# Moving all adaLN modulations to VectorE and regrouping attention into items of two score tiles

## The chip, the cores and the metric

The kernel runs on one core of one Trainium2 chip. The metric is the device time in microseconds (us) of one execution. TensorE (PE, with its weight loads as PEld), VectorE (DVE), ScalarE (ACT) and GpSimd (POOL) compute; SyncE (SP) issues the transfers from HBM.

## What is computed

One residual block on 256 tokens of width 1024 (a mixture of HGRN2, mLSTM and Mamba-2 branches, then a gated feed-forward with a depthwise convolution), a final norm, and then two layers of a second block on a latent stream of 256 tokens and a context stream of 256 tokens. All is float32. What matters here is the second block's modulation and its attention:

```python
def modulation(cond, w_ada, b_ada):
    m = jax.nn.silu(cond) @ w_ada + b_ada
    return [t[..., None, :] for t in jnp.split(m, 6, axis=-1)]

s_win = jnp.einsum('bnqhgd,bnkhd->bnhgqk', qb, kb).astype(jnp.float32) * scale
s_win = jnp.where(valid[None, :, None, None], s_win, -jnp.inf)
p = jax.nn.softmax(jnp.concatenate([s_win, s_ctx, s_sink], axis=-1), axis=-1)

p = jax.nn.softmax(s, axis=-1)
pd = p[:, :, 0] - lam * p[:, :, 1]
return jnp.einsum('bhqk,bkhd->bqhd', pd.astype(v.dtype), v)
```

The modulation of a layer is a product of two condition rows (one for the latent stream, one for the context) with a 1024 x 6144 matrix. The first softmax is that of 8 window heads of width 64 with 2 key heads, with a learned sink in the denominator; the last three lines are the 4 differential heads, each with two score maps of width 32 and values of width 64.

## The kernel before, in words

**Products.** Every weight tile (128 partitions x 1024 float32, 512 KB) is loaded by a transfer on SP's queue into the pool `wraw` of 4 buffers (`weight_raw`, L376), rounded on ScalarE to a high part `wh` (L383) and subtracted on VectorE to a low part `wl` (L385); both parts have 3 buffers. TensorE then makes the product in three passes (high x high L404, low activations L406, low weights L407; L429 to L431 for the projections that put tokens on partitions): 24 matmuls of 256 columns per weight in most stages. The scheduler orders each engine's instructions ahead of time, by the place in the program and with gaps filled by later work that is ready; buffers of a pool are handed out in program order, and a weight's load waits on SP's queue until the buffer that it takes is free. So the loads of the shared pool stand in the order of the program.

**Modulations.** A generator makes them in steps, and `ada_tick`, called after each weight (L417, L433, L634), runs one step each `pace` ticks. For layer 0 they are made on TensorE (`ada_pe`, L541 and L542): 12 blocks of 512 columns by 4 weights, each weight an ordinary `weight` (load, cast, subtract) and four matmuls of 512 columns with the condition rows as the stationary operand, then copies and small transposes (L528). They run from the mLSTM and SSD stage (`pace1` 2, set at L1190) through the first block's feed-forward (`pace3` 5, L1312), and what is left is run by `ada_rest()` behind that feed-forward (L1335). For layer 1, 40 blocks of 128 columns are made on VectorE (`ada_dve`, L571 to L582) during layer 0's feed-forward at `pace2` 1: a load into a pool of its own (`araw`, 3 buffers), and per condition one multiply-and-sum over 1024 elements (L580). Two blocks of 512 columns are left for TensorE, as filler in layer 1's attention (`afill`, L1677). `ada_rest()` stands behind layer 0's feed-forward too (L1728).

**Attention.** For each tile of 128 queries there are 12 items: 8 window heads, then 4 differential heads. `scores` runs two items ahead, `transposed` one ahead, and `values` last. A window head's scores are three matmuls over 64 array rows (L1517 to L1519) into a PSUM bank, with a mask matmul of 256 columns for latent tiles (L1521); then a maximum (L1523), a scaled maximum (L1525 or L1527), an exponential with sum (L1529), four transposes (L1562), a copy (L1564) and four products with the transposed probabilities as the stationary operand and 128 value columns of both key heads, of which 64 are used (L1574). A float32 matmul shows as two instructions in the trace. A differential head has two maps of 32 array rows, whose probabilities are combined (L1556). Latent tiles see 512 keys, context tiles 256. `OB` gathers the results with tokens on partitions; `finished` transposes six blocks of it and splits them into `XH` and `XL`. In layer 0 the context tiles run beside projections and the latent tiles beside the context's output products (`fill` says behind which items); in layer 1 only latent tiles remain.

Of the kernel before, what the change touches and what calls it, by code (L numbers as in the profile page):

```python
# [28 lines left out]
# columns of the modulations done on the tensor engine, 512 at a time, and on the vector engine, 128  # L29
ADA = ((range(0, 6144, 512), range(0)), (range(5120, 6144, 512), range(0, 5120, 128)))  # L30
# [3 lines left out]
# column offsets of the first block's w_in  # L34
# [4 lines left out]
# rows of the small projections: i gates, f gates, dt  # L39
# [3 lines left out]
def _ws(name, layer, c0, nk=8, r0=0):  # L43
    """[nk*128, 128] block of a weight, rows on partitions, 128 columns."""
    def cut(w):
        return w[name][layer][r0:r0 + nk * 128, c0:c0 + 128].reshape(nk, 128, 128).transpose(1, 0, 2)
    return nk * 128, cut


def _xs(name, layer, c0, half, cols=None):  # L50
    """[512, 256] block: rows on partitions, 256 columns that stream."""
    def cut(w):
        a = w[name][layer][half * 512:(half + 1) * 512]
        a = a[:, c0:c0 + 256] if cols is None else a[:, cols]
        return a.reshape(4, 128, 256).transpose(1, 0, 2)
    return 1024, cut


def _ada(layer, c0, q):
    """[256, 512] block: rows on partitions, 512 columns."""  # L60
    def cut(w):
        a = w["w_ada_2"][layer][q * 256:(q + 1) * 256, c0:c0 + 512]
        return a.reshape(2, 128, 512).transpose(1, 0, 2)
# [24 lines left out]
def _qcols(c):  # L88
    """256 columns of the window attention's queries, heads j and j + 4 side by side."""
    return np.concatenate([np.arange(512 + 64 * h, 576 + 64 * h) for h in HEADORDER[4 * c:4 * c + 4]])  # L90

# [33 lines left out]
def plan2(layer):  # L125
    p = [(("ada", c0, q), _ada(layer, c0, q)) for c0 in ADA[layer][0] for q in range(4)]
    p += [(("adat", c0), _adat(layer, c0)) for c0 in ADA[layer][1]]
# [8 lines left out]
    p += [(("out", j), _ws("w_out_2", layer, 128 * j)) for j in range(8)]  # L136
# [140 lines left out]
class Knobs:  # L277
    raw = 4
    wh = 3
    wl = 3  # L280
    big = 9
    araw = 3
# [17 lines left out]
def tile_two_blocks(ctx: ExitStack, tc: tile.TileContext, xT, ctxT, cst1, cst, cstw, pb1, pl0, pl1, pf0, pf1, pc, pcb, wb, w0, w1, out,  # L300
# [16 lines left out]
    class PS:  # L317
        """PSUM pools of the phase at hand"""

    def psum(**bufs):  # L320
        """Shares out the eight banks: name=number."""
# [3 lines left out]
        for nm in "asgcpo":  # L325
            if nm not in bufs:
                setattr(PS, nm, None)

    psum(g=3, s=4, a=1)
# [30 lines left out]
    ones = const.tile([128, 128], F32, name="ones")  # L360
    V.memset(ones, 1.0)
    onesn = const.tile([128, 128], F32, name="onesn")
# [30 lines left out]
    def gained(dst_h, dst_l, x, g):  # L393
        """x g, split: what the first products after a norm take; 1 / rms is applied to their results"""
# [4 lines left out]
    def mm3(o, w, rhs, nk, late=False, first=True, last=True):  # L399
        """o = W^T x in three passes; late: the low part of x comes last."""  # L400
# [11 lines left out]
    def gemm_ws(ph, key, rhs, n, nk=8, late=False, w=None):  # L412
        """out[128 features, n tokens] = W^T x; rhs(k) gives (high, low)."""
        w = w or weight(ph, key, 128)
        ps = PS.g.tile([128, 512], F32, tag="g", name="psg")
# [4 lines left out]
    def gemm_xs(ph, keys, lhs, toks, evac):  # L420
        """out[128 tokens, 256 features]; lhs(k, t) gives (high, low) of a token tile."""
        w = [weight(ph, k, 256) for k in keys]
        for t in toks:
            ps = PS.g.tile([128, 512], F32, tag="g", name="psx")
# [11 lines left out]
    def rsqrt_raw(pool, a, n, tag, bufs, rows=128):  # L436
        """RS * result = 1 / sqrt(a)"""
# [3 lines left out]
        # in two halves, so that neither waits for the step before  # L441
# [13 lines left out]
    def mean_sq(x, scale=None, eps=EPS):  # L455
        """mean of squares + eps, [128 tokens, 2 blocks of them], in PSUM"""
# [20 lines left out]
    def rms_all(a):  # L477
        """[128, 256] on every partition: 1 / (RS sqrt(a)) for tokens on partitions"""
# [19 lines left out]
    # =====================================================================  # L498
    # modulation: silu(c) w + b for both conditions, features on partitions
    # =====================================================================  # L500
    mods = [res.tile([128, 48, 2], F32, name="mod%d" % i) for i in range(2)]

    class Ada:
        pool = rows = None
# [5 lines left out]
    def ada_prep():  # L510
        zp = ctx.enter_context(tc.tile_pool(name="zp", bufs=1))
        Ada.cs = zp.tile([128, 8, 2], F32, name="ccs")
        Ada.cr = zp.tile([128, 8, 4], F32R, name="ccr")
        ct2 = zp.tile([128, 8, 2], F32, name="ct2")
        nc.sync.dma_start(out=ct2.rearrange("p k c -> p (k c)"), in_=pc)
        Ada.pf = [load_params(zp, _pf(i), (pf0, pf1)[i], "pf%d" % i) for i in range(2)]
        th = zp.tile([128, 8, 2], F32, name="cth")
        S.activation(out=th, in_=ct2, func=AF.Tanh, scale=0.5)
        V.scalar_tensor_tensor(th, th, 1.0, ct2, ALU.add, ALU.mult)
        V.tensor_scalar(Ada.cs, th, 0.5, None, ALU.mult)  # L520
        split(Ada.cr[:, :, 0:2], Ada.cr[:, :, 2:4], Ada.cs)

    def ada_pe(li):
        """512 columns at a time on the tensor engine; both parts of the conditions share a pass."""
        def finish(c0, rows):
            pt = PS.s.tile([128, 4, 4], F32, tag="s", name="psat")
            for q in range(4):
                T.transpose(pt[:, q], rows[q // 2][0:4, q % 2 * 128:q % 2 * 128 + 128], ident[0:4, 0:4])  # L528
            o = slice(c0 // 128, c0 // 128 + 4)
            V.tensor_tensor(mods[li][:, o], pt[:, :, 0:2],  # L530
                            Ada.pf[li]("bada")[:, o].unsqueeze(2).to_broadcast([128, 4, 2]), ALU.add)
            V.tensor_tensor(mods[li][:, o], mods[li][:, o], pt[:, :, 2:4], ALU.add)

        last = None
        for c0 in ADA[li][0]:
            ps = (PS.a or PS.s).tile([128, 512], F32, tag="s", name="psada")
            for q in range(4):
                wh, wl = weight(1 + li, ("ada", c0, q), 512)
                for kk in range(2):
                    k = 2 * q + kk  # L540
                    T.matmul(ps[0:4], Ada.cr[:, k], wh[:, kk], start=(k == 0), stop=False)  # L541
                    T.matmul(ps[0:2], Ada.cr[:, k, 0:2], wl[:, kk], start=False, stop=(k == 7))  # L542
                if last and q == 0:
                    finish(*last)
                if q < 3:
                    yield
# [1222 lines left out]
```

## Time and profile before

| what | us |
| --- | --- |
| runs | 1762.58, 1763.69, 1768.16 |
| median of the runs | 1763.69 |
| span of the profiled execution, first to last instruction | 1767.7 |
| TensorE busy in it | 1738.8 (98%) |
| VectorE busy in it | 1384.8 (78%) |
| ScalarE busy in it | 983.7 (56%) |

The profiled execution's own time is not given apart from its span; of the three runs it can only be the slowest, 1768.16 us, or one like it, so its span is 4.0 us over the median. The stages, in us from the span's start: HGRN2 to 245; mLSTM, SSD, branches and mixing 245 to 569; the first block's feed-forward 569 to 770; layer 0's projections and attention 770 to 1000, its feed-forward about 1015 to 1405; layer 1's projections to 1478, its attention to 1552, its output products and feed-forward to the end. A busy TensorE is not one at its peak, since the ends of matmuls are modelled; where matmuls follow each other, the distance of their starts is their cost.

### The profile page before, as it was taken

The page shows a single profiled execution, that of the slowest core. Times are in us where ns is not written, and L with a number is a line of the kernel's source. Part 1 is how long each engine was busy: PE and PEld are TensorE (multiplying, and loading weights), DVE is VectorE, ACT ScalarE, POOL GpSimd, SP SyncE. Part 2 cuts the span into 40 slices and gives each one's busy share as a digit, 9 for nine tenths or more (in the row PEclk, how much of TensorE's full clock was granted, in tenths as well). Part 3 has the DMA queues.
Part 4 walks back from the last instruction along what each step waited for, and adds up shares of the span by engine and source line. Part 5 has one row for each costly group of instructions (what it writes and reads, how often), then busy time and mean ns, then how long its engine had stood idle before and what let it go on. Part 6 is the DMA issues. An engine that isn't in the chain of part 4 may idle for free.

```text
span 1767.7 us, 31912 instructions
## 1 busy us (share of the span) xinstructions
PE 1738.8 (98%) x12442; PEld 1568.2 (89%) x12442; DVE 1384.8 (78%) x2716; ACT 983.7 (56%) x1723; POOL 0.2 (0%) x4
## 2 busy tenths in 40 slices
PE   7999999999999999999999999999999999999999
PEld 7999988878888999999878898888888997799999
DVE  7987967557778996877687799999656878788776
ACT  6655645445556865666676564442244556766554
POOL 0000000000000000000000000000000000000000
PEclk8999999999999999999989999999999999999999
DMA  7555445447677666654211356657433543046564
GB/s 233 159 154 152 138 132 157 147 126 222 218 228 228 187 190 221 209 170 139 86 67 47 105 163 189 183 171 232 129 96 107 168 132 120 24 141 195 174 196 132
DMA packets 80502, 276.97 MB, mean 157 GB/s; under 512 B 9056, under 2 KB 13792, under 8 KB 80224
## 3 DMA queue, kind: packets, MB, share of 16 engines
q1 hardware_dynamic: 80352, 274.94, 49.8%
q8 instruction: 98, 1.61, 0.4%
q14 instruction: 52, 0.43, 0.1%
HBM read 273.86 MB, written 1.05 MB: 156 GB/s over the span
## 4 chain that ended last, share of the span: by engine, by line
PE 51%; DVE 3%; ACT 1%; issue 0%; ACTq 0%
PE psg L404 12%; PE psg L407 12%; PE psg L406 11%; PE pso L1574 3%; PE psx L429 2%; PE psx L431 2%; PE psx L430 2%; PE psp L1562 2%; PE psc L1517 1%; PE psc L1519 1%; PE psc L1518 1%; DVE wl L385 0%; ACT Pp L1529 0%; DVE mx L1523 0%; PE psc L1521 0%
## 5 line engine op out<-in xcount | busy, mean ns | idle before, releaser
L383 ACT CAST wh<-raw 128x1024 fp32r<-128x1024 f32 (+1 forms) x475 | 490.9, 1037 | 531.0 <-PE psg L406 423.7
L385 DVE TENSOR_TENSOR wl<-raw,wh 128x1024 fp32r<-128x1024 f32 (+1 forms) x475 | 572.5, 1208 | 206.8 <-ACT wh L383 203.2
L404 PE MATMUL psg<-XH,wh 128*128 128x256 f32 (+1 forms) x1288 | 400.7, 314 | 3.6 <-ACT XH L390 1.9
L407 PE MATMUL psg<-XH,wl 128*128 128x256 f32 (+1 forms) x1288 | 398.8, 312 | 0.3 <-DVE wl L385 0.3
L406 PE MATMUL psg<-XL,wh 128*128 128x256 f32 (+1 forms) x1240 | 387.5, 313 | 0.7 <-DVE XL L1304 0.5
L404 PEld LDWEIGHTS psg<-XH,wh 128*128 128x128 f32 x1288 | 243.0, 189 | 22.0 <-ACT XH L390 2.3
L407 PEld LDWEIGHTS psg<-XH,wl 128*128 128x128 f32 x1288 | 243.3, 189 | 15.9 <-DVE wl L385 1.0
L406 PEld LDWEIGHTS psg<-XL,wh 128*128 128x128 f32 x1240 | 234.5, 189 | 16.1 <-DVE XL L1304 1.1
L404 PE MATMUL psg<-xh,wh 128*128 128x256 f32 x704 | 203.4, 289 | 1.8 <-ACT xh L390 1.3
L406 PE MATMUL psg<-xl,wh 128*128 128x256 f32 x704 | 200.5, 285 | 0.9 <-DVE xl L391 0.9
L407 PE MATMUL psg<-xh,wl 128*128 128x256 f32 x704 | 200.1, 284 | 0.3 <-DVE wl L385 0.3
L404 PE MATMUL psg<-hh,wh 128*128 128x256 f32 (+1 forms) x592 | 179.6, 305 | 0.1
L407 PE MATMUL psg<-hh,wl 128*128 128x256 f32 (+1 forms) x592 | 178.5, 302 | 0.0
L406 PE MATMUL psg<-hl,wh 128*128 128x256 f32 (+1 forms) x592 | 178.5, 302 | 0.0
L404 PEld LDWEIGHTS psg<-xh,wh 128*128 128x128 f32 x704 | 134.9, 192 | 6.0 <-ACT xh L390 1.5
L406 PEld LDWEIGHTS psg<-xl,wh 128*128 128x128 f32 x704 | 135.1, 192 | 2.9 <-DVE xl L391 1.4
L407 PEld LDWEIGHTS psg<-xh,wl 128*128 128x128 f32 x704 | 134.9, 192 | 2.2 <-issue 1.3
L406 PEld LDWEIGHTS psg<-hl,wh 128*128 128x128 f32 x592 | 111.5, 188 | 5.3 <-DVE hl L391 0.2
L404 PEld LDWEIGHTS psg<-hh,wh 128*128 128x128 f32 x592 | 110.9, 188 | 5.9 <-ACT hh L390 0.6
L407 PEld LDWEIGHTS psg<-hh,wl 128*128 128x128 f32 x592 | 111.2, 188 | 5.5
L429 PE MATMUL psx<-wh,XH 128*128 128x256 f32 x384 | 110.0, 287 | 1.1 <-DVE ss L1379 0.5
L430 PE MATMUL psx<-wh,XL 128*128 128x256 f32 x384 | 108.5, 283 | 0.0
(435 smaller groups left out, 3237.8 us busy)
## 6 DMA issues: line engine op xcount, KB each, us to landing
raw<-w SPq DMA_DIRECT2D x254, 512.0 KB, 3.7
raw<-wb SPq DMA_DIRECT2D x197, 512.0 KB, 4.3
araw<-w SPq DMA_DIRECT2D x40, 512.0 KB, 4.2
raw<-w SPq DMA_DIRECT2D x16, 384.0 KB, 3.4
raw<-wb SPq DMA_DIRECT2D x8, 384.0 KB, 3.2
xres<-xT SPq DMA_DIRECT2D x16, 128.0 KB, 3.6
plt<-pl SPq DMA_DIRECT2D x2, 588.0 KB, 5.5
xres<-ctxT SPq DMA_DIRECT2D x8, 128.0 KB, 2.7
```

What stands on the lines that cost most here:

```text
L383: S.copy(wh[:, 0:sz], raw[:, 0:sz])
L385: V.tensor_tensor(wl[:, 0:sz], raw[:, 0:sz], wh[:, 0:sz], ALU.subtract)
L404: T.matmul(o, wh[:, k], xh, start=(first and k == 0), stop=False)
L406: T.matmul(o, wh[:, k], xl, start=False, stop=False)
L407: T.matmul(o, wl[:, k], xh, start=False, stop=(last and not late and k == nk - 1))
L429: T.matmul(o, xh, wh[:, k % 4], start=(k == 0), stop=False)
L430: T.matmul(o, xl, wh[:, k % 4], start=False, stop=False)
L431: T.matmul(o, xh, wl[:, k % 4], start=False, stop=(k == 7))
L1517: T.matmul(o, qh, kh, start=True, stop=False)
L1518: T.matmul(o, qh, kl, start=False, stop=False)
L1562: T.transpose(ps[:, b], p[:, b * 128:(b + 1) * 128], ident)
L1574: T.matmul(po[:, i % 4], pt[:, b], v, start=(b == 0), stop=(b == nb - 1))
```

## The change

All 48 blocks of 128 columns of either layer are made by `ada_dve`, from loads in the shared pool `wraw` (`weight_raw`), with two steps (one per condition) for each load; so there are 96 steps per layer. The product of the first condition is written as bfloat16 (only its sum is used). `ada_rows`, which spreads the two condition rows over all partitions, is now run ahead of HGRN2 for layer 0 as well as ahead of layer 0's feed-forward for layer 1. `ada_pe`, its operands and the filler in layer 1 are gone. `pace1` and `pace2` stay 2 and 1, `pace3` goes from 5 to 2, and the context's norm asks for 32 steps in place of 17.

Attention has 8 items per tile: 4 pairs of window heads (one on array rows 0 to 63, the other on 64 to 127) and 4 differential heads. The score matmuls of an item's two tiles alternate, pass by pass, into two banks. The mask covers the 128 columns that need it. A pair's transposes fill up to two banks, and VectorE copies the second. In the window heads the 64 value columns are stationary and the transposed probabilities stream; the two heads of a pair write the lower and the upper 64 partitions of the same bank, so the result comes with features on partitions. The reciprocal sums are spread by 8 matmuls, copied by ScalarE and multiplied in by VectorE, and the split writes `XH` and `XL` directly; `finished` transposes two blocks. The rows of the output weights are permuted to match on the host. The banks of PSUM are shared out anew: layer attention has c=4, o=1, s=3 with the projections' tiles in s, in place of g=2, c=3, o=1, s=2 in layer 0 and c=4, o=1, s=2, a=1 in layer 1's attention; `fill` is chosen for 16 items.

The core of the diff (the parts of it that only take comments away are left out):

```diff
-ADA = ((range(0, 6144, 512), range(0)), (range(5120, 6144, 512), range(0, 5120, 128)))
+ADA = range(0, 6144, 128)
...
-    araw = 3
     pace0 = 1000
     pace1 = 2
     pace2 = 1
-    pace3 = 5
+    pace3 = 2
-    fill = (2, 6, 10, 14, 18, 22, 24, 26)
-    afill = tuple(range(20, 30))
+    fill = (1, 3, 6, 8, 11, 13, 15, 17)
...
     def ada_dve(li):
-        for c0 in ADA[li][1]:
-            o, sz = woff[1 + li][("adat", c0)]
+        for c0 in ADA:
             f = c0 // 128
-            raw = Ada.pool.tile([128, 1024], F32, tag="araw", name="araw", bufs=Knobs.araw)
-            nc.sync.dma_start(out=raw, in_=wsrc[1 + li][o:o + 128 * sz].rearrange("(p f) -> p f", p=128))
+            raw = weight_raw(1 + li, ("adat", c0))
             for c in range(2):
-                to = Ada.pool.tile([128, 1024], F32, tag="prod", name="prod", bufs=1) if c == 0 else raw
+                to = Ada.pool.tile([128, 1024], BF16, tag="prod", name="prod", bufs=1) if c == 0 else raw
                 V.tensor_tensor_reduce(to, raw, Ada.cb[:, c], 0.5, Ada.pf[li]("bada")[:, f:f + 1], ALU.mult, ALU.add,
                                        accum_out=mods[li][:, f, c:c + 1])
                 yield
...
-    Ada.pace, Ada.steps, Ada.rows = Knobs.pace0, ada_pe(0), p1
+    ada_rows(p1)
+    Ada.pace, Ada.steps = Knobs.pace0, ada_dve(0)
...
-        ada_steps(max(0, 17 - Ada.done))
+        ada_steps(max(0, 32 - Ada.done))
...
-        psum(g=2, c=3, o=1, s=2)
+        psum(c=4, o=1, s=3)
...
+            for q_, k_, n in ((qkh, qkh, 0), (qkh, qkl, 1), (qkl, qkh, 2)):
+                for e, (d, jq, jk, h, _) in enumerate(rows):
+                    T.matmul(ps[e][:, 0:A.nk], q_[d, jq, A.tq], k_[d, jk, kk], start=(n == 0),
+                             stop=(n == 2 and not mask))
+            if mask:
+                o = slice(128 * (1 - A.t), 128 * (1 - A.t) + 128)
+                for e in range(2):
+                    T.matmul(ps[e][:, o], identb, winb[:, A.t, o], start=False, stop=True)
...
+                if i:
+                    V.tensor_copy(pt[:, 0:len(some)], ps[:, 0:len(some)])
+                else:
+                    S.copy(pt[:, 0:len(some)], ps[:, 0:len(some)])
...
+            if i < 4:
+                for b in range(nb):
+                    for e in range(2):
+                        d = slice(64 * e, 64 * e + 64)
+                        T.matmul(po[d, i], BV[:, kb0 + b, d], pt[e][b], start=(b == 0), stop=(b == nb - 1))
+            if i == 3:
...
+                for j in range(4):
+                    for e in range(2):
+                        T.matmul(ps[64 * e:64 * e + 64, j], es[:, 2 * j + e:2 * j + e + 1].to_broadcast([128, 64]),
+                                 ident, start=True, stop=True)
+                rs = ap.tile([128, 512], F32, tag="scr", name="rsb", bufs=Knobs.scr)
+                S.copy(rs, ps.rearrange("p j q -> p (j q)"))
+                V.tensor_tensor(rs, rs, po.rearrange("p j q -> p (j q)"), ALU.mult)
+                r4 = rs.rearrange("p (j q) -> p j q", j=4)
+                split(XH[:, 2:6, A.tm], XL[:, 2:6, A.tm], r4)
...
-            psum(c=Knobs.c1, o=1, s=6 - Knobs.c1, a=1)
-            Ada.steps, Ada.rows = ada_pe(1), None
-            for i, _ in enumerate(seq(gmlp(0), attention((1, 0)))):
-                if i in Knobs.afill:
-                    ada_steps(1)
-            ada_rest()
+            for _ in seq(gmlp(0), attention((1, 0))):
+                pass
```

## Rows read from the trace of the kernel before

**Rows 1.** The page, first part: busy time of each engine over the span.

```profile
PE 1738.8 (98%) x12442; PEld 1568.2 (89%) x12442; DVE 1384.8 (78%) x2716; ACT 983.7 (56%) x1723; POOL 0.2 (0%) x4
```

**Rows 2.** Windows: start:end length, busy us (instructions) by engine, PEclk, DMA share, GB/s.

```profile
245.00:569.00 324.00, 320.13 (x2314) 272.86 (x2314) 222.88 (x380) 172.43 (x307) 0.00 (x0) 0.99 0.58 183
...
569.00:770.00 201.00, 198.56 (x1624) 190.74 (x1622) 169.56 (x309) 129.14 (x208) 0.00 (x0) 1.00 0.64 200
...
1045.00:1255.00 210.00, 210.00 (x924) 170.74 (x923) 203.51 (x301) 76.43 (x98) 0.00 (x0) 1.00 0.61 188
...
1255.00:1405.00 150.00, 150.00 (x837) 129.78 (x835) 94.80 (x137) 65.07 (x91) 0.00 (x0) 1.00 0.38 120
...
1357.00:1405.00 48.00, 48.00 (x399) 47.71 (x398) 39.96 (x70) 26.59 (x43) 0.00 (x0) 1.00 0.52 165
...
1478.00:1552.00 74.00, 72.94 (x481) 53.70 (x480) 52.69 (x152) 49.77 (x109) 0.00 (x0) 1.00 0.20 62
```

**Rows 3.** Groups by line and shape: the first of two modulation matmuls: busy us, mean ns, idle before.

```profile
L541 PE MATMUL psada<-wh,ccr 128*4 128x512 f32 x112 | 44.5, 398 | 1.6 <-ACT wh L383 1.6
```

**Rows 4.** TensorE timeline, one weight of the modulations: start us, us, operation.

```profile
704.08 0.40 PE L541 MATMUL psada<-wh,ccr 128*4 128x512 f32 x1
...
704.99 0.28 PE L404 MATMUL psg<-XH,wh 128*128 128x256 f32 x1
```

**Rows 5.** Groups by line and shape on VectorE: weight subtract, and modulation product.

```profile
L385 DVE TENSOR_TENSOR wl<-raw,wh 128x1024 fp32r<-128x1024 f32 x451 | 549.7, 1222 | 193.5 <-ACT wh L383 190.2
...
L580 DVE CUSTOM_DVE_ANT_0 prod<-araw,ccb,pf 128x1024 f32<-128x1024 f32 x40 | 51.1, 1278 | 0.0
```

**Rows 6.** VectorE timeline around one modulation product.

```profile
1060.05 1.28 DVE L580 CUSTOM_DVE_ANT_0 araw<-araw,ccb,pf 128x1024 f32<-128x1024 f32 x1
...
1061.25 0.69 DVE L660 TENSOR_TENSOR av<-ag,av 128x512 f32<-128x512 f32 x1
```

**Rows 7.** SP timeline, weight loads around the end of the first feed-forward.

```profile
755.84 16.66 SPq L376 DMA_DIRECT2D raw<-w  x7
```

**Rows 8.** TensorE timeline, one window head of a latent tile, first layer.

```profile
958.51 0.49 PE L1517 MATMUL psc<-qkh 64*128 64x512 f32 x1
...
959.52 0.61 PE L1574 MATMUL pso<-CV,PT 128*128 128x128 f32 x4
...
962.11 0.60 PE L1562 MATMUL psp<-ct,Pp 128*128 128x128 f32 x4
...
962.54 1.06 PE L1574 MATMUL pso<-CV,PT 128*128 128x128 f32 x8
...
963.35 0.36 PE L404 MATMUL psg<-XH,wh 128*128 128x256 f32 x1
```

**Rows 9.** TensorE timeline, one differential head of a latent tile, second layer.

```profile
1501.70 0.50 PE L1517 MATMUL psc<-qkh 32*128 32x512 f32 x2
...
1502.89 0.63 PE L1562 MATMUL psp<-ct,Pp 128*128 128x128 f32 x4 [0.22 <-DVE Pp L1556]
...
1504.34 0.51 PE L1517 MATMUL psc<-qkh 32*128 32x512 f32 x2
```

**Rows 10.** TensorE timeline at the gated MLP: matmuls of 64 stationary columns on column halves.

```profile
826.55 0.28 PE L430 MATMUL psx<-wh,XL 128*128 128x256 f32 x1
...
826.67 0.28 PE L431 MATMUL psx<-wl,XH 128*128 128x256 f32 x1
...
826.88 1.09 PE L1497 MATMUL psmix<-plt,AV 128*64 128x128 f32 x16
```

**Rows 11.** Groups by line and shape: score maxima, exponentials and a copy of transposes.

```profile
L1523 DVE TENSOR_REDUCE mx<-psc 128x1 f32<-128x512 f32 x64 | 43.6, 686 | 21.2 <-PE psc L1521 13.7 <-PE psc L1519 6.9
...
L1529 ACT ACTIVATE Pp<-psc,nm,ss 128x512 f32<-128x512 f32 x64 | 49.6, 778 | 9.9 <-DVE nm L1525 4.5 <-DVE nm L1527 4.2 <-DVE vnt L447 0.8
...
L1564 ACT COPY PT<-psp 128x512 f32<-128x512 f32 x48 | 28.0, 586 | 24.1 <-PE psp L1562 23.8
```

**Rows 12.** Windows: a stretch of the first layer's attention, columns as in group 2.

```profile
900.00:920.00 20.00, 18.49 (x94) 14.69 (x93) 15.52 (x46) 13.40 (x31) 0.00 (x0) 0.74 0.25 80
```

More of the change, by code (lines that the diff above doesn't have):

```diff
@@ L90, in _qcols, with _mixrows @@
     return np.concatenate([np.arange(512 + 64 * h, 576 + 64 * h) for h in HEADORDER[4 * c:4 * c + 4]])
+def _mixrows():
+    heads = [np.arange(256 + 64 * h, 320 + 64 * h) for h in HEADORDER]
+    return np.concatenate([np.arange(256), *heads, np.arange(768, 1024)])
 def _ffn_plan(up, down, layer):
@@ L125, in plan2 @@
 def plan2(layer):
-    p = [(("ada", c0, q), _ada(layer, c0, q)) for c0 in ADA[layer][0] for q in range(4)]
-    p += [(("adat", c0), _adat(layer, c0)) for c0 in ADA[layer][1]]
+    p = [(("adat", c0), _adat(layer, c0)) for c0 in ADA]
     for h in range(2):
@@ L135, in plan2 @@
     p += [(("au", j), _ws("w_in_2", layer, 128 * j)) for j in range(2)]
-    p += [(("out", j), _ws("w_out_2", layer, 128 * j)) for j in range(8)]
+    p += [(("out", j), _ws("w_out_2", layer, 128 * j, rows=_mixrows())) for j in range(8)]
     p += _ffn_plan("w_up_2", "w_down_2", layer)
@@ L503, in tile_two_blocks @@
     class Ada:
-        pool = rows = None
         ticks = 0
@@ L519, in ada_prep @@
[L519 to L546, printed above, removed]
-            rows = [Ada.rows.tile([128, 256], F32, tag="arow", name="arow", bufs=2) if Ada.rows is not None else
-                    tmp.tile([128, 256], F32, tag="t256", name="arow", bufs=6) for _ in range(2)]
-            for e in range(2):
-                S.copy(rows[e][0:4], ps[0:4, e * 256:(e + 1) * 256])
-            last = (c0, rows)
-            if Ada.rows is None:
-                finish(*last)
-                last = None
-            yield
-        if last:
-            finish(*last)
-            yield
@@ L645, in ffn @@
                     w = [weight(ph, ("up", e // 2, e % 2), 128) for e in range(3)]
-                    first = [PS.g.tile([128, 512], F32, tag="g", name="psg") for _ in range(3)]
+                    first = [PS.g.tile([128, 512], F32, tag=PS.gtag, name="psg") for _ in range(3)]
                     for c in reversed(H):
@@ new lines, in scores @@
+            ps = [PS.c.tile([128, 512], F32, tag="c", name="psc") for _ in range(2)]
+            kk = slice(A.k0, A.k0 + A.nk)
+            mask = i < 4 and A.t < 2
+            for q_, k_, n in ((qkh, qkh, 0), (qkh, qkl, 1), (qkl, qkh, 2)):
[6 more added lines that the diff above has]
+                    T.matmul(ps[e][:, o], identb, winb[:, A.t, o], start=False, stop=True)
@@ L1559, in transposed @@
[L1559 to L1567 removed]
+            return pp[:1]
+        def transposed(A, pp):
+            out = []
+            blocks = [(p, b) for p in pp for b in range(A.nb)]
+            for i in range(0, len(blocks), 4):
+                some = blocks[i:i + 4]
+                ps = PS.s.tile([128, 4, 128], F32, tag="s", name="psp")
+                for n, (p, b) in enumerate(some):
+                    T.transpose(ps[:, n], p[:, b * 128:(b + 1) * 128], ident)
+                pt = ap.tile([128, 4, 128], F32, tag="PT", name="PT", bufs=Knobs.ptb)
+                if i:
+                    V.tensor_copy(pt[:, 0:len(some)], ps[:, 0:len(some)])
+                else:
+                    S.copy(pt[:, 0:len(some)], ps[:, 0:len(some)])
+                out += [pt[:, n] for n in range(len(some))]
+            return [out[j:j + A.nb] for j in range(0, len(out), A.nb)]
@@ L1617, in attention @@
                 A.tm = slice(mcol(t), mcol(t) + 128)
-                items += [(A, i) for i in range(12)]
+                items += [(A, i) for i in range(8)]
             n = len(items)
```

170 lines of the change are left out of this document (70 added, 100 removed).

## The prediction

> **What bounds the kernel now.** I read the busy shares first. TensorE is busy 98% of the span, VectorE 78%, ScalarE 56% [rows 1]: one engine is full nearly everywhere, so work taken off TensorE counts only where no other engine is close behind. The windows by stage say where that is [rows 2]. From 245 to 569 us VectorE is busy 223 us of 324, with 101 free. In the first feed-forward (569 to 770) it has 170 of 201, so 31 free. From 1045 to 1255, where the modulations of layer 1 already run on VectorE, it has 204 of 210 while TensorE never idles. From 1255 to 1405 it has 95 of 150, and in the last down products within that of layer 0's feed-forward (1357 to 1405) it has 40 of 48. In layer 1's attention (1478 to 1552) it has 53 of 74. So the reader should see a kernel bound by TensorE, with VectorE as the next limit in both feed-forwards.
>
> **Part 1, modulations leave TensorE.** One weight of them costs TensorE 704.99 - 704.08 = 0.91 us [rows 4]; with its share of the small transposes and copies about 1.05. L541 has 112 matmuls [rows 3] and L542 one beside each, four to a weight, so 56 weights, 48 for layer 0 and 8 for layer 1. By the ticks, 72 come between 245 and 569 at one weight per two, so 36 weights x 1.05 = 38 us lie there, 12 weights (12 us) in the first feed-forward, and 8 weights (8 to 10 us) in layer 1's attention.
>
> What VectorE gives and takes: each weight loses a subtract of 1.22 us and ScalarE a cast. Each step is a multiply-and-sum of 1.28 us [rows 5], of which the next instruction sees 1061.25 - 1060.05 = 1.20 [rows 6]; with the reading of its sum I take 1.25. Layer 0 now has 96 steps, 36 of them between 245 and 569 (72 ticks, pace 2). There 36 x 1.25 = 45 comes and 36 x 1.22 = 44 goes, so VectorE's sum stays at 224 while TensorE's falls to 320 - 38 = 282. Even so 58 us stay free on VectorE; I take **-34** of the 38, bounds -18 (many of these matmuls only stood in for waits) and -38.
>
> In the first feed-forward 68 ticks at pace 2 give 34 steps, and **26 steps are left for `ada_rest()`** behind it (96 - 36 - 34). VectorE's work between 569 and 770 becomes 170 - 12 x 1.22 + 60 x 1.25 = 230 us, in a stage of 201. TensorE's 12 us less are worth nothing there. The 26 steps (32 us) come in the program ahead of the final norm and of the second block's weights, and since their 13 loads take buffers of the shared pool in order, the next weights' loads stand behind them on SP's queue. Today the first of those are issued at 755.84 us, some 14 us ahead of their use at about 770 [rows 7]. What hides part of the lump is the three finished weights that TensorE still has, about 3 x 24 x 0.118 = 8.5 us (0.12 us per matmul [rows 10]), less the cast and subtract of the first new weight (about 3). I take **+28**: 230 - 201 = 29 as the bound by the sum, +24 and +35 as ends.
>
> For layer 1: 73 ticks at pace 1 give 73 steps in layer 0's feed-forward and leave **23 steps for the second `ada_rest()`**. Today the 80 steps have their own buffers and are done at 1255, far ahead of their ticks; in the shared pool a load can be only some seven weights ahead. So 16 steps now fall into the last 48 us: 40 + 16 x 1.25 + 23 x 1.25 = 89 us of VectorE's work where 48 are. The excess is 41; about 11 of it (some seven weights' lead, four loads and three finished weights, at 1.25 each, and a little more) can start earlier, beside the products before 1357, where VectorE has room [rows 2]. I take **+30**, ends +20 and +41. The 16 casts and subtracts of layer 1's 8 weights and their filler belong to attention below. ScalarE's share only falls.
>
> `ada_rows` now also runs ahead of HGRN2: 8 small VectorE and 8 ScalarE instructions of 256 columns, about 4 us each, and a transfer of 1 MB, beside projections: **+2** (0 to +4). The waits of some 25 us behind each lump let TensorE's clock fall; the trace has one stretch where it did, with a granted clock of 0.74 in the mean of 20 us [rows 12]: about half of it at 1.2 GHz in place of 2.4, which cost 0.26 x 20 = 5 us of full-speed work. The stretch behind a lump restarts with dense products, so I take **+3** for both (0 to +10).
>
> **Part 2, attention.** A window head of a latent tile costs TensorE 959.52 - 958.51 = 1.01 us for scores and mask, 962.54 - 962.11 = 0.43 for transposes and 963.35 - 962.54 = 0.81 for values [rows 8]: 2.25, so 4.5 for two. A pair: scores of both tiles on different rows at once, 1.01 if they run together; eight transposes 0.86; values of both heads at once on column halves, 0.81. That they do is bounded by two rows: the two maps of a differential head already show as "x2" in one line, and its whole item takes 1504.34 - 1501.70 = 2.64 us with 0.22 idle for VectorE [rows 9]; and the 16 matmuls of 64 stationary columns take 1.09 us, 64 to 68 ns each against 0.81 / 8 = 101 for full width [rows 8, 10]. Going into the column halves costs 826.88 - 826.67 = 0.21 in place of 0.12 [rows 10], 0.09 each way. Sum 2.68 + 0.18 = 2.9, a gain of 1.6 per pair, 6.4 per tile of four. Spreading the sums takes 16 instructions (1 us), of which four transposes saved return 0.4; the mask and maps that now always start together return 0.5 to 1.5. So about 6.5 us per latent tile and half of it per context tile.
>
> VectorE and ScalarE per pair: two maxima 1.37, a copy about 0.6 and small ones 0.3, so 2.3; two exponentials 1.56 with their sums' reading 0.4 and a copy 0.59 [rows 11], so 2.5. Both are under 2.9 but close. Layer 0, two latent and two context tiles: 19.5 at most, beside projections and output products that take up slack; I take **-17** (-8 to -22). Layer 1: 13 and the filler of 8 to 10, less the waits that the filler covered; **-18** (-8 to -23).
>
> The Trainium skill, page "TensorEngine Tiling (Array Packing)", section "PSUM Bottleneck", says that tiling speeds up TensorE and not the copies out of PSUM, which may then limit. By that rule, with the copies' waits on top of ScalarE's 2.5 us, a pair would go at some 3.3 us in place of 2.9, the gain of the 16 latent pairs would shrink by 16 x 0.4 = 6 us, and the sum would be 0 instead of -6; the rows, with both engines still under TensorE, speak for -6.
>
> **Sum.** -34 + 28 + 30 + 2 + 3 - 17 - 18 = -6, or 1767.7 - 6 = 1762 by the profiled span. That span is 4.0 over the median of the runs, 1763.7; set against the median the forecast is **1758**. This likeliest case by itself runs from 1740 to 1776.
>
> **Rivals.**
>
> *The lumps are hidden.* If the steps spread over VectorE's free time (101 us from 245 to 569, 55 from 1255 to 1405 [rows 2]) or the next weights' loads pass them, +28, +30 and +3 go: 1758 - 61 = 1697; with half of them hidden 1727. For it: the steps of layer 1 run ahead of their ticks today. Against it: that was with buffers of their own. Chance 0.18.
>
> *The modulations were filler (slower).* The matmuls of 245 to 569 stand where TensorE would wait for the chains of the mLSTM and SSD branches; then taking them away gives back only waits. At a gain of 8 in place of 34 the time is 1758 + 26 = 1784, at none 1792. It decides from a gain under 24 us, where the time passes 1763.7 + 5. For it: ScalarE and VectorE both alternate with TensorE there. Against it: after the change TensorE still has 282 of 290 us, and VectorE 224. Chance 0.2.
>
> *Attention gains nothing.* The two tiles of a pair or the two column halves run one after the other, or items go at the pace of their waits (3.3 us and more per pair): -35 becomes -15, of which the filler is most, so 1758 + 20 = 1778. It would also show as a lower clock: where TensorE's work is thin the granted clock was 0.74 [rows 12], and a quarter to half of layer 1's some 60 us of matmuls at the lower level would cost 15 to 30 us by itself. The Trainium skill, page "TensorE: Matmul & The Clock Gate", part 1, says that throttled is the default and that activity releases it; by that rule less work in the same attention means more of it at 1.2 GHz, and the rows at 0.74 agree. Chance 0.12.
>
> **How the numbers follow.** The likeliest case keeps 0.5. A measurement of this kernel can tell about 0.3%, 5.3 us, from no change: 1758.4 to 1769.0. Of the 0.5, 0.25 lies below, 0.16 within and 0.09 above. Lumps hidden add 0.18 to faster; filler adds 0.02 to faster, 0.02 to same and 0.16 to slower; attention 0.01 to same and 0.11 to slower. Faster 0.45, same 0.19, slower 0.36. The range leaves out the lowest part of the hidden lumps (0.1) and the highest of the slower cases (0.1): 1712 to 1790.
>
> **What would show it.** Right: no L541; modulation products at a steady one per two weights, then some 26 and some 23 of them in a row; TensorE idle 20 us and more before the first `psx` of either layer, released by `wl` L385 or `wh` L383; the stage now at 245 to 569 shorter by about 34; pairs of L1517 in one line and window pairs near 2.9 us. Wrong: a stage of 245 to 569 that stays within 15 us of 324, no idle before the projections, or a granted clock near 0.5 through layer 1's attention.

## The result and the profile after

The changed kernel takes 1813.66 us in the median of 4 runs (1810.57 to 1817.10), the kernel before in the same comparison 1765.93. The ratio is 1.026, with an interval of 1.023 to 1.029: **slower by 48 us**, where 1758 was forecast, and outside the range of 1712 to 1790. The profiled span is 1813.1 us, against 1767.7.

Two rows of the first part of the page answer to [rows 1]:

```profile
span 1813.1 us, 31392 instructions
...
PE 1666.2 (92%) x12234; PEld 1530.0 (84%) x12234; DVE 1447.3 (80%) x2841; ACT 912.9 (50%) x1615; POOL 0.2 (0%) x4
```

TensorE is busy for 72.6 us less (1738.8 - 1666.2), as planned, and yet the end is later by 45.4 us of span: so some 118 us of idle time are new. To see where, I cut both traces at the same products (the n-th first-pass matmul of a weight, which both kernels run in about the same order), so that a stage holds the same weights in both. The windows of the kernel before, cut in this way (start:end and length, busy us of PE, PEld, DVE, ACT and POOL, granted clock, DMA share, GB/s; the stages are the mixers; the first feed-forward up to the first projection of layer 0; layer 0's projections and attention; its output products and feed-forward up to layer 1's projections; layer 1's projections and attention; the cut into this last stage lies 9 us behind its first product in either kernel):

```profile
199.20:553.80 354.60, 352.50 (x2597) 305.82 (x2596) 249.85 (x420) 187.64 (x334) 0.00 (x0) 0.99 0.57 177
553.80:770.50 216.70, 212.11 (x1729) 202.79 (x1727) 181.31 (x337) 138.88 (x223) 0.00 (x0) 1.00 0.65 202
770.50:1017.40 246.90, 243.77 (x1804) 216.65 (x1805) 186.12 (x553) 162.44 (x349) 0.00 (x0) 0.97 0.30 97
1017.40:1414.20 396.80, 396.25 (x2062) 336.61 (x2061) 329.85 (x512) 163.46 (x235) 0.00 (x0) 1.00 0.51 159
1414.20:1554.80 140.60, 138.91 (x1024) 116.20 (x1023) 103.76 (x283) 86.84 (x180) 0.00 (x0) 1.00 0.29 91
```

The same stages in the changed kernel, which answer to [rows 2]:

```profile
199.10:521.40 322.30, 319.11 (x2424) 293.33 (x2423) 247.55 (x442) 150.24 (x283) 0.00 (x0) 0.99 0.53 169
521.40:784.10 262.70, 210.75 (x1678) 206.23 (x1677) 236.74 (x459) 131.63 (x214) 0.00 (x0) 0.91 0.63 201
784.10:1030.90 246.80, 222.32 (x1828) 198.11 (x1829) 178.10 (x504) 144.42 (x311) 0.00 (x0) 0.93 0.29 91
1030.90:1467.00 436.10, 398.85 (x2069) 339.25 (x2069) 355.77 (x561) 166.81 (x243) 0.00 (x0) 0.96 0.51 157
1467.00:1601.50 134.50, 123.37 (x1002) 105.94 (x1001) 92.31 (x257) 72.08 (x156) 0.00 (x0) 0.94 0.20 64
```

Read the lengths against each other, and length less PE busy as TensorE's idle time:

| stage | length, us | forecast | idle before | idle after |
| --- | --- | --- | --- | --- |
| mixers | -32.3 | -34 | 2.1 | 3.2 |
| first feed-forward and first lump | +46.0 | +28 | 4.6 | 52.0 |
| layer 0's projections and attention | -0.1 | -17 | 3.1 | 24.5 |
| layer 0's output, feed-forward, second lump | +39.3 | +30 | 0.6 | 37.3 |
| layer 1's projections and attention | -6.1 | -18 | 1.7 | 11.1 |

What lies before the first cut changes by -0.1 us, where +2 was forecast for `ada_rows`, and what lies behind the last by -1.3.

The first lump is plain to see. In the 32 us behind the first feed-forward VectorE never rests and TensorE works for 5 us, at a mean clock of 0.61 (window, columns as above):

```profile
745.00:777.00 32.00, 4.92 (x31) 4.66 (x29) 31.98 (x61) 6.77 (x12) 0.00 (x0) 0.61 0.62 194
```

What TensorE waits for there is not the next weight, as I had it, but the sums of squares of the final norm, which stand between the modulation steps on VectorE. The TensorE timeline (start, duration, operation, idle time before and what ended it):

```profile
746.63 0.28 PE L406 MATMUL psg<-hh,wl 128*128 128x256 f32 x1
759.27 0.58 PE L464 MATMUL psn<-onesn,sacc 128*128 128x1 f32 x2 [12.37 <-DVE sacc L472]
...
775.85 0.56 PE L464 MATMUL psn<-onesn,sacc 128*128 128x1 f32 x2 [14.71 <-DVE sacc L472]
...
782.48 1.19 PE L481 MATMUL psr<-ct,rcy 128*128 128x128 f32 x4 [4.78 <-DVE rct L446]
784.13 0.58 PE L428 MATMUL psx<-wh,XH 128*128 128x256 f32 x1 [0.46 <-ACT rr L483]
```

The norm's chain (4.8 us for the root) stands ahead of the first projection too; in the kernel before the projection began without it.

The pairs themselves do nearly what was forecast. One pair of window heads of a latent tile in layer 1's attention, in a stretch at a granted clock of 1.00, with its scores at 1572.05, its transposes at 1573.06 and its values at 1574.04, to be set against [rows 8] (2.25 us per head):

```profile
1572.05 0.50 PE L1486 MATMUL psc<-qkh 64*128 64x512 f32 x2
...
1573.06 1.04 PE L1525 MATMUL psp<-ct,Pp 128*128 128x128 f32 x8
1574.04 1.09 PE L1544 MATMUL pso<-PT,BV 128*64 128x128 f32 x16
1575.06 0.50 PE L1486 MATMUL psc<-qkh 32*128 32x512 f32 x2
```

The pair takes 1575.06 - 1572.05 = 3.0 us where 2.9 was forecast: 1.01 for the scores of both tiles, as forecast, 0.98 for the transposes (0.86) and 1.02 for the sixteen value matmuls, 64 ns each (0.81 and 0.18 for the change to column halves). So TensorE's saving of some 1.5 us a pair is there, and layer 0's attention still ends no earlier. The waits of TensorE in that stage (total us, times, longest) name the places:

```profile
PE pso L1583 <- DVE OB L1578: 8.8, 4, 6.1
PE pst L1418 <- DVE QK L1403: 5.7, 1, 5.7
PE psmix L1448 <- DVE AV L1440: 2.4, 1, 2.4
```

### The profile page after: what moved, and what is told of

Read it like the earlier page. It is cut to its first block, busy times and chain, and to the rows that moved or that the text cites. A ratio compares the mean times of both kernels' runs of the same rounds, so it can differ in the third digit from the quotient of the medians.

```text
span 1813.1 us, 31392 instructions
## 1 busy us (share of the span) xinstructions
PE 1666.2 (92%) x12234; PEld 1530.0 (84%) x12234; DVE 1447.3 (80%) x2841; ACT 912.9 (50%) x1615; POOL 0.2 (0%) x4
## 4 chain that ended last, share of the span: by engine, by line
PE 62%; DVE 21%; DMA 8%; issue 5%; ACT 4%; SPq 0%; ACTq 0%; DVEq 0%
PE psg L403 14%; PE psg L406 14%; PE psg L405 14%; DVE wl L384 6%; DMA raw<-w 5%; PE psx L428 3%; PE psx L430 3%; PE psx L429 3%; DMA raw<-wb 2%; ACT wh L382 2%; DVE prod L530 2%; DVE raw L530 2%; PE psl L819 1%; DVE mx L1499 1%; PE psc L1486 1%
## 5 line engine op out<-in xcount | busy, mean ns | idle before, releaser
L382 ACT CAST wh<-raw 128x1024 fp32r<-128x1024 f32 (+1 forms) x419 | 432.8, 1036 | 467.4 <-PE psg L405 310.0
L384 DVE TENSOR_TENSOR wl<-raw,wh 128x1024 fp32r<-128x1024 f32 (+1 forms) x419 | 504.0, 1206 | 135.6 <-ACT wh L382 133.3
L530 DVE CUSTOM_DVE_ANT_0 prod<-raw,ccb,pf 128x1024 bf16<-128x1024 f32 x96 | 123.1, 1283 | 72.8 <-DMA raw<-w 72.4
L530 DVE CUSTOM_DVE_ANT_0 raw<-raw,ccb,pf 128x1024 f32<-128x1024 f32 x96 | 122.8, 1280 | 0.1
```

The lines of the kernel that those rows point to most:

```text
L382: S.copy(wh[:, 0:sz], raw[:, 0:sz])
L384: V.tensor_tensor(wl[:, 0:sz], raw[:, 0:sz], wh[:, 0:sz], ALU.subtract)
L530: V.tensor_tensor_reduce(to, raw, Ada.cb[:, c], 0.5, Ada.pf[li]("bada")[:, f:f + 1], ALU.mult, ALU.add, accum_out=mods[li][:, f, c:c + 1])
```

## The experiments

Twelve kernels, in three sets; each set was timed against the kernel before on its own chip (medians 1767.93, 1765.86 and 1767.02 us). Ratios are to that, with their 95% intervals.

### Which part loses

**The attention alone.** Modulations of layer 0 as before; all 48 blocks of layer 1 on VectorE with buffers of their own, since the filler in layer 1's attention would blur it.

```diff
-ADA = ((range(0, 6144, 512), range(0)), (range(5120, 6144, 512), range(0, 5120, 128)))
+ADA = ((range(0, 6144, 512), range(0)), (range(0), range(0, 6144, 128)))
```

> The new attention with the old modulations of layer 0 (TensorE); layer 1's 96 steps all on VectorE with buffers of their own, no filler in its attention. The theory that the attention gives its saved TensorE work back by itself (waits on the chains of VectorE and ScalarE and a lower clock) expects the two attentions together within 10 us of the kernel before: 1755 to 1767 us. The rival, that its waits are the aftermath of the lumps of modulation steps, expects most of the 35 us: 1730 to 1745 us.

Measured: 1780.77 us, ratio 1.0067 (1.0044 to 1.0089). Worse than either theory: the attention change does not only give its saving back, it loses 13 us by itself. The lumps are no part of it. By stage, from windows cut as above: layer 0's attention 245.9 us (before 246.9), layer 1's 133.7 (140.6), but the first feed-forward with the step to the projections 230.5 (216.7), and layer 0's output products and feed-forward 404.2 (396.8).

**The modulations alone,** with the old attention.

> The new modulations with the old attention. By the ledger of the two traces (work of 245 to 569 us down 32, first feed-forward up 10, first lump up 34, layer 0's feed-forward up 5, second lump up 34, filler of layer 1 gone 8 to 10 down) the theory expects about 40 us over the kernel before, 1800 to 1812 us. The rival, that the attention change carries the loss, expects 1780 us or less.

Measured: 1808.28 us, ratio 1.0222 (1.0197 to 1.0248), as the theory had it: 40 us of the 48 belong to the modulations. Mixers 321.9 us (-32.7), first feed-forward and lump 253.0 (+36.3), layer 0's projections and attention 251.9 (+5.0), its feed-forward and lump 433.4 (+36.6), layer 1's attention 137.9 (-2.7). Here the projections have banks of their own, as before, and the wait behind the first feed-forward is the forecast one: from the last product at 745.6 us to the first projection at 773.2, half of it for the norm's sums and half for the next weight's high part, whose load came behind the steps' (waits of TensorE, 700 to 774 us):

```profile
PE psx L418 <- ACT wh L372: 13.1, 1, 13.1
PE psn L454 <- DVE sacc L462: 12.6, 1, 12.6
```

### The lumps

**Buffers of their own for layer 1's loads,** all else as changed.

```diff
-            raw = weight_raw(1 + li, ("adat", c0))
+            if li:
+                o, sz = woff[1 + li][("adat", c0)]
+                raw = Ada.pool.tile([128, 1024], F32, tag="araw", name="araw", bufs=3)
+                nc.sync.dma_start(out=raw, in_=wsrc[1 + li][o:o + 128 * sz].rearrange("(p f) -> p f", p=128))
+            else:
+                raw = weight_raw(1 + li, ("adat", c0))
```

> The changed kernel, but layer 1's modulation loads go to three buffers of their own as in the kernel before; the tick rate is the same. If the second lump comes from the shared pool's order (loads of the steps stand in line with the weights), the steps run ahead into VectorE's free time and the second lump goes: 30 to 34 us less than the changed kernel, 1780 to 1784 us. If it comes from the number of steps left at the end of the ticks or from VectorE's sum, nothing moves: 1808 us or more.

Measured: 1777.5 us, ratio 1.0054 (1.0034 to 1.0074), 36 us less than the changed kernel. The stage with the second lump falls from 436.1 to 400.2 us:

```profile
1035.70:1435.90 400.20, 395.14 (x2068) 336.85 (x2068) 354.94 (x561) 167.60 (x243) 0.00 (x0) 1.00 0.55 170
```

VectorE does the same 355 us of work in it as in the changed kernel's stage (355.8), and the ticks are the same. What it no longer does is wait for these loads: 39.3 us in the changed kernel's stage (the line is in the last section), none here. So it was neither VectorE's sum nor the 23 steps left over at the end of the ticks: in the shared pool the steps cannot run ahead. The edit does two things at once, it takes these loads out of the weights' order and it adds three buffers; a shared pool of seven was not tried, so that the order alone does it is not shown.

**The steps spread over the ticks,** in the shared pool.

```diff
-    pace1 = 2
+    pace1 = 1
-    pace3 = 2
+    pace3 = 3
...
-            ada_steps(1)
+            ada_steps(2 if Ada.more and Ada.ticks % 3 == 0 else 1)
```

> The changed kernel with the steps spread over the ticks: every tick from 245 to 569 us, every third in the first feed-forward, four per three ticks in layer 0's feed-forward, so that both end-of-stage calls have two steps or none left. If the two lumps are the loss (68 us by the ledger) and VectorE has room elsewhere: 1740 to 1760 us. If VectorE's sum bounds the stages, the time only moves into them: 1790 us or more.

Measured: 1769.5 us, ratio 0.9999 (0.9978 to 1.0021), 10 us above the band that I gave. The first lump goes: the first feed-forward with the step to the projections takes 228.7 us in place of 262.7, while the mixers, with some 34 more steps in them by the trace (71 and 37), take 324.8 (322.3). The second mostly stays: its stage takes 422.6 us in place of 436.1, where buffers of their own gave 400.2. So each lump has its own cure: the free time of VectorE before the first feed-forward takes layer 0's steps, and own buffers take layer 1's.

**Both cures together.**

> The changed kernel with both cures for the lumps: layer 0's steps at every tick from 245 to 569 us and every third in the feed-forward (two left), layer 1's loads in three buffers of their own. By the ledgers of the two single cures (first feed-forward 37 us less, second lump 36 us less): 1738 to 1748 us, faster than the kernel before, with the attention's idle time of 21 us still in it. If the two cures share a cause: 1760 us or more.

Measured: 1746.06 us, ratio 0.9880 (0.9861 to 0.9899). They add up: 33 us and 36 us less in the two stages with a lump (229.3 and 400.2), 67.6 in the median.

**The modulations alone with both cures,** and the old attention.

> The modulations-alone kernel (old attention) with both cures of the lumps. By the ledgers (1808 us less 34 and 34): 1738 to 1750 us, so that the modulations on VectorE are by themselves a gain of some 20 us. If the lumps' work only moves into other stages with the old attention: 1755 us or more.

Measured: 1729.06 us, ratio 0.9784 (0.9756 to 0.9811), better than expected. So the modulations on VectorE are worth 38 us, and the new attention, as it was changed, takes 17 us of them back (1746 - 1729). The two stages with attention, for the comparison with the last kernel below:

```profile
746.40:990.90 244.50, 241.00 (x1805) 213.88 (x1806) 185.61 (x553) 162.38 (x349) 0.00 (x0) 0.97 0.32 98
...
1382.60:1521.80 139.20, 134.08 (x984) 114.58 (x983) 95.40 (x272) 78.72 (x169) 0.00 (x0) 0.95 0.20 61
```

### The attention's waits

The waits named above are for VectorE's chains; the question is why TensorE has no projection to work on meanwhile. PSUM's eight banks are shared out by use: c for scores, o for results, g for projections, s for the rest. In the changed kernel the projections draw their PSUM banks from s, the three banks that the transposes, the norms and the spreading of sums rotate through.

**Two banks for the projections.** The attention-alone kernel, first with g=2, c=2, o=1, s=3:

```diff
-        psum(c=4, o=1, s=3)
+        psum(g=2, c=2, o=1, s=3)
...
+            psum(c=4, o=1, s=3)
             for _ in seq(gmlp(0), attention((1, 0))):
                 pass
```

> The attention-alone kernel with two PSUM banks given back to the projections: g=2, c=2, o=1, s=3 in place of c=4, o=1, s=3 with the projections in s; in layer 1 the banks become c=4, o=1, s=3 for the attention itself. Theory: a projection's bank stands in the rotation of s behind banks that wait for VectorE's chains, so TensorE's new idle time in layer 0's projections and attention (21 us) and ahead of them (6 us) comes from the sharing; then 1750 to 1765 us, though c=2 holds only one pair of scores. Rival, that the pairs' own chains (exponential, copy, values, spreading of the sums) make the waits: 1776 us or more.

Measured: 1759.33 us, ratio 0.9964 (0.9953 to 0.9974), 21 us less than the attention alone. The wait in front of the transposes of `OB`, 8.8 us before, is nearly gone, though s still has three banks and c has lost two:

```profile
PE pso L1640 <- DVE OB L1635: 0.2, 1, 0.2
```

Then with the old kernel's g=2, c=3, o=1, s=2:

> As the kernel before it, with the banks of the kernel before: g=2, c=3, o=1, s=2 (layer 1's attention c=4, o=1, s=3). Theory of the shared banks: 1750 to 1765 us, the waits named for the split of transposed queries and keys (qkl) in front of projections gone; with s=2 a pair's two banks of transposes fill s, so some of it may return. Rival: 1776 us or more.

Measured: 1754.81 us, ratio 0.9940 (0.9924 to 0.9957), 26 us less. The waits in layer 0's projections and attention that are left, all that are over 0.3 us:

```profile
PE pst L1476 <- DVE QK L1471: 2.6, 3, 1.3
PE pst L1476 <- DVE qkl L400: 1.1, 1, 1.1
PE psx L438 <- DVE xres L1325: 0.4, 1, 0.4
PE pso L1640 <- DVE OB L1635: 0.4, 2, 0.2
```

The 8.8 us in front of the transposes of `OB` and the 5.7 for `QK` are gone, with the same chains on VectorE. And the first projection no longer waits for the final norm. In the attention-alone kernel TensorE ends the feed-forward and then waits its way through the norm:

```profile
774.78 0.36 PE L474 MATMUL psn<-onesn,sacc 128*128 128x1 f32 x2
...
780.25 0.59 PE L474 MATMUL psn<-onesn,sacc 128*128 128x1 f32 x2 [3.10 <-DVE sacc L482]
...
783.84 1.19 PE L491 MATMUL psr<-ct,rcy 128*128 128x128 f32 x4 [1.72 <-DVE rcy L460]
785.49 0.58 PE L438 MATMUL psx<-wh,XH 128*128 128x256 f32 x1 [0.46 <-ACT rr L493]
```

With banks of its own the projection starts 0.8 us behind the first of these sums (10.7 us above):

```profile
770.98 0.36 PE L474 MATMUL psn<-onesn,sacc 128*128 128x1 f32 x2
771.75 0.36 PE L438 MATMUL psx<-wh,XH 128*128 128x256 f32 x1 [0.41 <-DVE xres L1325]
```

**A slower interleave,** the rival for the 6 us at the end of the context tiles (`ra` 4 to 2):

> The attention-alone kernel with two in place of four attention steps behind each step of the latent projections (the items are fewer and larger now, so that four of them run out sooner). If the waits at the end of the context tiles (6 us in front of the transposes of OB) come from attention that has run out of projections to stand beside: 1768 to 1775 us. If the shared banks make the waits: within 5 us of 1781 us.

Measured: 1780.51 us, ratio 1.0077 (1.0061 to 1.0093), the same as the attention alone. The wait for `OB` falls from 8.8 to 3.8 us, but 3.5 us of waits for exponentials, where there were 0.9, are there too, and no time is won: the rate of the interleave moves the waits and is not what costs the 26 us.

**The banks in the changed kernel.**

> The changed kernel, with lumps and all, and only the projections' banks given back. If the sharing costs as much here as in the attention-alone kernel (26 us): 1786 to 1792 us. If part of it is hidden by the first lump (the final norm and the projections wait for VectorE anyway): 1795 to 1805 us.

Measured: 1793.7 us, ratio 1.0158 (1.0130 to 1.0187), 20 us less than the changed kernel, between the two bands. The part at the final norm is partly hidden by the first lump: the stage with it gains 6.6 us (262.7 to 256.1), where it gained 13.3 without a lump (230.5 to 217.2).

**One bank of their own,** on the kernel with both cures (g=1, c=4, o=1, s=2):

> As the first of these, but g=1, c=4, o=1, s=2: one bank of their own for the projections, and score banks for two pairs. If pairs that can start together are worth what c=3 loses (work in layer 0's attention fell by 24 us with c=4 and by 9 with c=3): 1705 to 1718 us. If one bank for the projections makes each wait for its copy: 1725 us or more.

Measured: 1744.64 us, ratio 0.9874 (0.9848 to 0.9901): no gain in sum over the same kernel without it (1746). One bank is enough to end the wait at the final norm (the first feed-forward's stage takes 218.4 us in place of 229.3) and nearly all of that for `OB`, with four banks for scores as in the changed kernel. But with one bank projections wait for the copy of the one before, and layer 1's projections and attention take 141.2 us in place of 133.0. The waits of TensorE in layer 0's projections and attention:

```profile
PE psx L428 <- ACT QK L1347: 7.7, 9, 1.3
PE psx L428 <- ACT AV L1365: 3.3, 2, 2.2
PE psg L403 <- ACT AU L1361: 3.0, 3, 1.3
...
PE pso L1588 <- DVE OB L1583: 0.7, 2, 0.5
```

**Everything together:** both cures, and g=2, c=3, o=1, s=2.

> The spread steps with layer 1's own buffers, and the projections' banks given back (g=2, c=3, o=1, s=2, and c=4, o=1, s=3 for layer 1's attention). If the banks' 26 us and the lumps' cures add up: 1718 to 1726 us. If the idle time in layer 0's attention is only moved once VectorE also carries the steps: 1735 us or more.

Measured: **1714.92 us** (1713.38 to 1716.06), ratio 0.9708 (0.9686 to 0.9731), faster than either kernel: 52 us under the one before, 99 under the changed one, and 3 better than the band. All stages are shorter than before, but for the second with 1.3 us more:

```profile
202.20:528.10 325.90, 320.77 (x2425) 293.39 (x2423) 283.69 (x503) 150.81 (x283) 0.00 (x0) 0.99 0.61 192
528.10:746.10 218.00, 203.10 (x1661) 200.25 (x1659) 194.56 (x374) 126.43 (x203) 0.00 (x0) 0.97 0.64 202
746.10:982.30 236.20, 231.06 (x1848) 199.78 (x1849) 183.22 (x528) 149.52 (x322) 0.00 (x0) 0.98 0.32 99
982.30:1377.50 395.20, 392.92 (x2067) 335.47 (x2066) 350.67 (x553) 165.24 (x240) 0.00 (x0) 1.00 0.56 172
1377.50:1505.20 127.70, 118.59 (x1003) 102.34 (x1002) 95.93 (x265) 74.00 (x159) 0.00 (x0) 0.97 0.23 67
```

The new attention is worth 14 us here (1729.06 - 1714.92).

## Why the prediction was wrong

By the spans the forecast missed by 51 us (+45.4 against -6). Of these 27 lie in the two stages with a lump and 29 in the two with attention; the other terms make up -5.

**Right:** the mixers' stage. -34 was forecast, -32.3 came, and the same with the old attention (-32.7). The rival that the modulation matmuls were only filler falls. The place of both lumps, behind the two feed-forwards, held as well, and so did the length of the waits themselves: with the old attention 27.6 us from the end of the feed-forward to the first projection, in each of the two places, where the forecast's own items for the first give 26.5 (32 of steps, less 8.5, and 3). That the shared pool keeps layer 1's steps from running ahead was foreseen too.

**Mis-sized: what VectorE's load costs in the two feed-forwards.** In the modulations-alone kernel the stages with the lumps lose 36.3 and 36.6 us, against 28 and 30. For the first, the step that failed is "TensorE's 12 us less are worth nothing there": they were worth less than nothing. The feed-forward takes 225.4 us to its last product, and before the change 215.9, though it holds 12 us less of TensorE's work. The kernel before, then the modulations-alone kernel to its last product, in its lump and in the products behind it (windows, columns as above):

```profile
553.80:769.70 215.90, 211.68 (x1726) 202.46 (x1724) 180.88 (x336) 138.22 (x222) 0.00 (x0) 1.00 0.65 203
...
520.20:745.60 225.40, 206.29 (x1658) 202.36 (x1657) 201.29 (x384) 123.66 (x201) 0.00 (x0) 0.96 0.64 201
745.60:773.20 27.60, 1.93 (x10) 1.82 (x9) 27.60 (x53) 5.31 (x10) 0.00 (x0) 0.54 0.62 191
773.20:782.00 8.80, 7.09 (x31) 6.71 (x32) 7.85 (x26) 2.09 (x2) 0.00 (x0) 0.51 0.72 221
```

TensorE's idle time in the feed-forward rises from 4.2 to 19.1 us, and the granted clock falls from 1.00 to 0.96. The changed kernel's waits of TensorE in that stage name weight subtracts and convolution taps on VectorE, which cost 0.3 us and nothing before the change:

```profile
PE psg L406 <- DVE wl L384: 5.6, 7, 2.2
...
PE psg L403 <- DVE ag L575: 4.0, 3, 1.8
```

That these come late because modulation steps of 1.28 us stand in front of them is argued from the order on VectorE, not tested by itself; with 26 steps in the feed-forward in place of 37, and no lump, the stage takes 217.4 us (the modulations alone with both cures). The forecast let VectorE's sum set the length of the stage with its lump; in the run VectorE is busy 228.9 of these 253.0 us, since it also waits for others. Of the second stage's 36.6 us some 27 are the lump, 4 the products behind it up to the cut, at the lower clock, and 6 the feed-forward itself; what these 6 are was not taken apart.

The clock behind the lumps was put at 3 us for both. In the modulations-alone kernel the products behind the first lump run for 8.8 us, and those behind the second for 8.2, at a granted clock of 0.51 and 0.50, the lower of the two levels, with TensorE busy 7.1 and 6.4 us of them. Half of that, some 7 us, is what the clock costs there, an estimate.

**Wrong: the attention,** -17 and -18 forecast, -0.1 and -6.1 measured, with a loss at the final norm on top (13.8 us in the attention-alone kernel's stage). The forecast's step costed each pair's instructions, nearly rightly (2.9 against 3.0 us), and then took the saving off a stage bound by TensorE as if nothing else changed there. It passed over the one line of the diff that shares out the banks anew, though the text ahead of it tells of that line. In its place the runs showed that projections which share s with the transposes and norms leave TensorE waiting for VectorE's chains: two banks of their own take 21 and 26 us off the attention alone, and the waits for `OB` and at the final norm go in each of the three splits tried (g=2, c=2, s=3; g=2, c=3, s=2; g=1, c=4, s=2). So it is not the number of banks in s or in c that ends them. What exactly orders TensorE's queue within the shared rotation was not taken apart.

Even with the banks given back the attention is worth 14 us and not 35. Against the same modulations with the old attention, layer 0's stage falls by 8.3 us (244.5 to 236.2), where 17 was forecast, and layer 1's by 11.5 (139.2 to 127.7), which covers the 8 to 10 left there without the filler; some 4 us go back elsewhere, most of them in layer 0's output products and feed-forward (391.7 to 395.2). The filler was mis-sized: taking it away gives 1.4 to 2.7 us (140.6 to 139.2 and 137.9) where 8 to 10, less the waits it covered, were counted. Why layer 0's attention gives only half is only argued: with c=3 the two tiles of a pair can't always start together. It fits that TensorE's busy time in this stage falls by 21.5 us with c=4 (243.8 to 222.3) and by 9.9 with c=3 (241.0 to 231.1).

**The two slower rivals that I wrote** were on the right side, but neither had the mechanism. That the modulations were filler is refuted. *Attention gains nothing* was the nearer one, at a chance of 0.12, but as a matter of tiles that don't run at once or of the clock. The clock is part of it as a consequence: it is lower where TensorE idles, with a mean of 0.91 in the stage of the first lump and 0.93 in layer 0's attention, against 1.00 and 0.97 before. The Trainium skill, page "TensorE: Matmul & The Clock Gate", part 1, has throttling as the default that activity lifts; the trace agrees, with 0.54 in the lump of 27.6 us above and 1.00 in the dense feed-forward of the kernel before. The Trainium skill, page "TensorEngine Tiling (Array Packing)", section "PSUM Bottleneck", says that copies out of PSUM may come to limit. No run shows that for the attention's own copies, which the prediction weighed at 6 us: the pair above takes 3.0 us and not 3.3. In the kernel with one bank for the projections TensorE does wait for ScalarE's copies, but of projections.

## What to carry to other kernels

Work moved to an engine with free time gains only if its loads can run ahead into that time: give them buffers of their own, or place the steps where the engine is free, and count what is left at each forced end. When a change touches the split of PSUM banks, list for each product whose release it will wait for, before costing a single instruction; here two banks for the products that fill gaps turned a new attention that lost 17 us into one that gains 14. Test the parts alone: here one part held a gain of 38 us and the other one of 14, behind faults of placing that cost 99 us together.

## What the runs showed of the hardware that was not expected

Spreading costs little where an engine looks nearly full: in the last kernel VectorE is busy 283.7 of 325.9 us in the mixers, with some 34 more steps than in the changed kernel, and the stage is only 3.6 us longer than that one's (322.3).

VectorE stood for modulation loads in the changed kernel, which it did not before. Its waits in layer 0's output and feed-forward, up to layer 1's projections (total us, times, longest):

```profile
DVE prod L530 <- DMA raw<-w: 39.3, 18, 4.5
```

VectorE does nothing else in these 39.3 us, in the very stage whose end waits for VectorE; with buffers of their own that wait is gone and the stage is 36 us shorter.
